# A two-layer decoder trunk on one core: other PSUM banks at a stage's end, one transposed piece and one small sum moved

## The chip, the cores and the metric

The kernel runs on one core of one Trainium2 chip. A core has TensorE (PE, with its weight loads shown as PEld), VectorE (DVE), ScalarE (ACT), GpSimd (POOL) and SyncE (SP), each with its own queue of instructions in a fixed order; they wait for each other by semaphores. Matmul results go to PSUM, which this kernel uses as eight banks of 128 x 512 float32. The metric is the time of one execution on the device, in microseconds (us).

## The reference

The input x has 256 tokens of 2048 channels, the memory 256 of the same width. All values are float32. Cut to what matters here:

```python
for i in range(2):
    if i == 1:                       # shared keys and values, from the stream after layer 0
        kv = rms_norm(x, kv_norm) @ w_kv
        k1, k2 = (partial_rope(rms_norm(k, k_norm)) for k in the first two column parts of kv)
        v = the rest of kv
    u = rms_norm(x, mix_norm[i]) @ w_in[i]
    if i == 0:  token_out = pooled means of u (windows 2, 4, 8, 16), one map for each group
    else:       token_out = differential attention of 12 heads with k1, k2, v
    q = rms_norm(the last 512 columns of u, by head)            # 4 memory heads of 128
    mem_out = softmax(q @ mem_k.T / sqrt(128)) @ mem_v           # for each head
    x = x + concat(token_out, mem_out) @ w_out[i]
    z = relu(rms_norm(x, ffn_norm[i]) @ w_ff1[i])                # 8192 wide
    x = x + (z * z) @ w_ff2[i]
```

## The kernel before

**Products.** Each float32 operand is split into a high part (rounded to fp32r) and a low part (the rest). A product is three matmuls: high by high, low by high, high by low. Weights come in rows of blocks in the order of use. `Feed` loads them (SP's queue), makes the high part with a cast on ScalarE (L199) and the low part with a subtraction on VectorE (L202), into a ring of slots, and does so up to three pieces of weights ahead of their use (`AHEAD`). A slot is free again when the matmuls that read it are done. The instructions of each engine are put in a fixed order before the run by a planner, which goes by the order of the program and by what it estimates to be ready.

**Small work between.** `at(d, fn)` puts a piece of work d steps ahead; `tick()` makes a step, after every four blocks of weights (a quad).

**Feed-forward stage** (`ffn`, once in each layer). 64 tiles of the first product (`up_tile`) go one after the other through the single bank of tag "st" (x_bank, copied out by L863). Between them stand jobs of the second product, computed with a scheme of seven products for two times two blocks; these hold the seven other banks: three of tag "mm", two of "s", one of "o", one of "t". When the left half of the output is done, it is turned back in four pieces (`turn_left`): four transposes into the "st" bank (L1020), a copy to SBUF (`evict`, L816), an add to the residual stream (L1028). `turns` holds the pieces; one is taken before each of the last up tiles, the fourth before tile 63. After tile 63, `last()` makes the last twelve jobs, eight, two and two of them ahead of output tiles 0, 1 and 2 (`down_tile`). After the last job, `finish_banks` combines the seven banks on VectorE (L1040 to L1048) and turns the right half back in four pieces (L1059, L1060). Output tiles 0 to 2 use the "st" bank, tiles 3 to 7 the three "mm" banks in turn; VectorE reads those from the bank (L891) and adds them (L892). As each chunk of the stream is finished, it is scaled and split into x_kv (L450 on ScalarE, L368 on VectorE).

**Keys and values.** Right behind, three tiles of keys and three of values are computed from x_kv, then two tiles for the memory. Each takes 16 steps, one for each chunk of x_kv; a step is `wide_step`, three products (L506, L507, L508) for each half of the tokens, and a bank for each half. `pair_of_banks(c, ...)` gives the two banks. The first key tile takes the chunks in the order `ready`, the others from 0 to 15.

**Queries of layer 1.** Three tiles of attention queries, and then four memory queries, one for each head. `mem_query` squares a head's query and, in `stats`, two steps later, sums the squares over the head's width by small matmuls into the "st" bank (L667); VectorE (L672) and ScalarE make the scale y of them. `mem_head` computes the scores four steps after the query, the exponentials with y (L699) and their scaling (L706), turns them four steps later (L712), and multiplies by the values after another four. The attention heads turn their outputs back through the "st" bank as well (`back`, L1545).

Of the kernel before, what the change touches and what calls it, by code (L numbers as in the profile page):

```python
# [10 lines left out]
F32 = mybir.dt.float32  # L11
# [6 lines left out]
P = 128  # L18
T = 256
NK = 16  # L20
# [310 lines left out]
def program(ctx, tc, plan, dry, xT, memT, par, lam, cst, wst, yT):  # L331
# [5 lines left out]
    pp = ctx.enter_context(tc.tile_pool(name="pp", bufs=1, space=PSUM))  # L337
# [10 lines left out]
    def at(d, fn, rank=1):  # L348
        pend.setdefault(now[0] + d, []).append((rank, fn))

    def tick():
        now[0] += 1
        for _, fn in sorted(pend.pop(now[0], []), key=lambda x: x[0]):
            fn()
# [6 lines left out]
    def vt(name):  # L361
        return tp.tile([P, T], F32, tag="v", bufs=6, name=name)

    def mmt(name):
        return pp.tile([P, 512], F32, tag="mm", bufs=3, name=name)

    def stt(out, a, s, b, op0, op1, **kw):
        return nc.vector.scalar_tensor_tensor(  # L368
            out=out, in0=a, scalar=s, in1=b, op0=op0, op1=op1, **kw
        )  # L370
# [44 lines left out]
    def gcol(c):  # L415
        return param[:, c : c + 1]
# [13 lines left out]
    def rsqrt_cols(out, v, parts=None):  # L430


        n = v.shape[-1]
        w = [tp.tile([P, 16], F32, tag="w8", bufs=8, name="rc")[:, :n] for _ in range(4)]
        if parts:
            for t in range(2):
                x, s, b = parts(t)
                nc.scalar.activation(w[0][:, t : t + 1], x, AF.Ln, scale=s, bias=b)
        else:
            nc.scalar.activation(w[0], v, AF.Ln)  # L440
        nc.scalar.activation(w[1], w[0], AF.Exp, bias=lnc, scale=-0.5)
        nc.vector.tensor_mul(w[2], w[1], w[1])
        nc.vector.tensor_mul(w[3], w[2], v)  # L443
        stt(out, w[3], 3.0 * CN * CN, w[1], ALU.subtract, ALU.mult, reverse0=True)

    def stat(name):
        return pp.tile([P, T], F32, tag="st", bufs=1, name=name)
# [64 lines left out]
    def b_tile(ps, w, l, c, xs):  # L512
        for k in range(NK):
            wide_step(ps, (w, l, k, c, 4), xs, k)

    def map_tile(ps, w, l, blocks, xs, ks=range(NK)):

        for k in ks:
            wide_step(ps, [(w, l, k, n, 1) for n in blocks], xs, k, ks)
# [132 lines left out]
    def mem_query(src, gq, cols):  # L652


        q = vt("mq")
        sq = vt("mq_sq")
        ql = tp.tile([P, T], F32R, tag="acc", bufs=1, name="mq_lo")
        q = q.bitcast(F32R)
        nc.scalar.activation(sq, src, AF.Square)
        nc.scalar.activation(q, src, AF.Copy, scale=gq)  # L660
        stt(ql, src, gq, q.bitcast(F32), ALU.mult, ALU.subtract)
        y = tp.tile([P, 2], F32, tag="m2", bufs=12, name="mq_y")

        def stats():
            st = stat("st_mq")
            for t in range(2):
                nc.tensor.matmul(  # L667
                    st[:, 2 * t : 2 * t + 2], sq[:, t * P : t * P + P], ones_h,
                    start=True, stop=True,
                )  # L670
            v2 = tp.tile([P, 2], F32, tag="m2", bufs=12, name="mq_v")
            nc.vector.tensor_mul(v2, st[:, 0:4].rearrange("p (a b) -> p a b", b=2)[:, :, 0], cols[1])  # L672
            nc.vector.tensor_scalar_add(v2, v2, EPS)
            rsqrt_cols(y, v2)
            nc.vector.tensor_mul(y, y, cols[0])

        at(2, stats)
        return (q, ql), y

    def mem_head(q, y, k, v, e, pT, out, lag, pv_lag=6, tag="s"):  # L680
# [88 lines left out]
    def ffn(l, xs, tags, done):  # L769
# [136 lines left out]
        def bank():  # L906
            return pp.tile([P, 512], F32, tag="st", bufs=1, name="x_bank")
# [13 lines left out]
        def slab_jobs(g, i, again, end):  # L921
            k = 2 * i
            first = 2 if g == 0 else 0
            n = feed.slab(
                [
                    [("w_ff2", l, k, c, 4), ("w_ff2", l, k + 1, c, 4)]
                    for c in (first, first + 1)
                ]
            )

            def side(b):
                assert i in done_pairs
                return [pair(i)[:, e, b * P : b * P + P] for e in range(2)]

            sides = (
                ((0, A11), (1, A12)),
                ((2, S1),),
                ((3, S2), (4, S4)),
                ((5, S3), (6, A22)),
            )  # L940

            def run(j):
                hi, lo = feed.job(n, j)
                for c, (p, a) in enumerate(sides[j]):
                    s = slice(512 * c, 512 * c + 512)
                    assert holds[p] == g
                    product(p, g, end, side(a), hi[:, s], lo[:, s])
                feed.job_used(n, j)
                if j == 3 and not again and i < 28:
                    pair_free[i % 5] = True  # L950

            return run
# [19 lines left out]
        def swap(j, g):  # L972
            for p in of_job[j]:
                x = keep.pop(0)
                nc.scalar.copy(x, banks[p])
                saved[1 - g, p] = x
                restore(p, g)

        left = {}
        turns = []  # L980
# [92 lines left out]
        jobs = [(s, j) for s in range(len(slabs)) for j in range(4)]  # L1073
        runs = {}

        def one_job():
            s, j = jobs.pop(0)
            g, i, again = slabs[s]
            end = s + 1 == len(slabs) or slabs[s + 1][0] != g
            if j == 0:  # L1080
                runs[s] = slab_jobs(g, i, again, end)
            runs[s](j)
            if end and s + 1 < len(slabs):
                if g == 1 and i == 27:
                    at(1, lambda: close_left(j))
                else:
                    at(3 if j == 3 else 2, lambda: swap(j, 1 - g))
# [7 lines left out]
        def due(tiles, least=0):  # L1095
            n = 0
            while len(jobs) > 12:
                s, j = jobs[0]
                if tiles_at(s) + j * (tiles_at(s + 1) - tiles_at(s)) / 4 > tiles and n >= least:
                    break  # L1100
                one_job()
                n += 1
# [5 lines left out]

        for i in range(4, 64):
            due(i, 2)  # L1110
            if turns:
                turn_left(turns.pop(0))
                due(i, 2)
            up_tile(i, bank(), lambda b, i=i: due(i + b / 16) if b > 0 and b % 4 == 0 else None)
        due(64)
        assert len(jobs) == 12 and not turns
        feed.loads_ahead = LOADS

        def last():
            for n in range(8):  # L1120
                for _ in range((8, 2, 2, 0, 0, 0, 0, 0)[n]):
                    one_job()
                    tick()
                if n == 2:
                    finish_banks()
                if n == 7:
                    feed.in_ffn, feed.more = False, None
                down_tile(n, bank() if n < 3 else mmt("ff2"))
# [80 lines left out]
    for i in range(2):  # L1209
        c = slice(2 * i, 2 * i + 2)  # L1210
# [21 lines left out]
    ps = [mmt("mq0"), pp.tile([P, 512], F32, tag="o", bufs=1, name="mq0")]  # L1232
# [12 lines left out]
    for i in range(2):  # L1245
        c = slice(2 * i, 2 * i + 2)
# [145 lines left out]
    nc.vector.tensor_scalar_mul(qcol, gcol(G_QN), 0.125)  # L1392

    def pair_of_banks(c, name):
        if c % 2:
            return [pp.tile([P, 512], F32, tag="s", bufs=2, name=name) for _ in range(2)]
        return [mmt(name) for _ in range(2)]

    c1 = []
    at(14, lambda: c1.extend(columns("x")))  # L1400
    for c in range(3):
        ps = pair_of_banks(c, "k1")
        ready = [0, 1, 2, 3, 4, 5, 8, 9, 10, 11, 6, 12, 13, 14, 15, 7] if c == 0 else range(NK)
        map_tile(ps, "w_kv", 0, (2 * c, 2 * c + 1, 6 + 2 * c, 7 + 2 * c), x_kv, ready)
        rows = key_rows(ps, c1, 64)
        rope(rows, ktab)
        for i in range(2):
            at(
                9,
                lambda i=i, c=c, rows=rows: turn_rows(  # L1410
                    rows, 2 * i, kT[:, 4 * c + 2 * i : 4 * c + 2 * i + 2, :], gcol(G_KN)
                ),
            )
    for c in range(3):
        ps = pair_of_banks(c + 1, "v1")
        b_tile(ps, "w_kv", 0, 3 + c, x_kv)
        for t in range(2):
            nc.scalar.activation(
                vv[c][:, t, :], ps[t], AF.Copy, scale=c1[0][:, t : t + 1]
            )  # L1420
# [3 lines left out]
    ps = pair_of_banks(0, "mk1")  # L1424
    b_tile(ps, "w_mem_kv", 1, 0, mems1)
    mrow1 = key_rows(ps, mem_c, P)
    ps = pair_of_banks(1, "mv1")
# [11 lines left out]
    for i in range(2):  # L1439
        c = slice(2 * i, 2 * i + 2)  # L1440
# [114 lines left out]
    for c in range(3):  # L1555
        ps = pair_of_banks(0, "q1")
# [4 lines left out]
        for i in range(2):  # L1561
            j = 2 * c + i
# [11 lines left out]
    for h in range(4):  # L1574
        ps = mmt("mq1")
# [106 lines left out]
```

## Time and profile before

| | |
|---|---|
| median of 3 runs | 2002.17 us (2001.77 to 2003.84) |
| profiled execution, its own time | 2003.26 us |
| its span, first to last instruction | 2001.5 us |
| mean granted TensorE clock | 0.999 |
| busy: PE, DVE, ACT, POOL | 1990.5, 1730.7, 1456.2, 157.7 us |
| read from HBM | 418.00 MB, 210 GB/s over the span |

Rows of the order of time give the start, the duration, the engine, the line, the operation, what it writes and reads with its shape, and how many instructions the row holds; in brackets stands how long the engine was idle just before, and which instruction ended that. A row of waits gives the engine and line that waited, the one waited for, and then the total in us, the number of times and the longest. Starts of neighbouring matmuls lie closer than their durations, since they overlap. A row by stretches ends with the granted clock, the share of DMA and GB/s.

### The profile page before, as it was taken

The numbers are of one execution on the slowest core, as the hardware profiler recorded it, in microseconds if no ns is written. First come the engines' busy times: TensorE is split into PE (matmuls) and PEld (weight loads), VectorE is DVE, ScalarE is ACT, GpSimd is POOL, SyncE is SP. The second block draws the span as 40 slices with busy tenths as digits, with TensorE's granted clock in tenths as the row PEclk, the third lists the DMA queues.
The fourth block names the chain that finished last, engine by engine and source line by source line (L and its number), as shares of the span: only waits on it lengthen the run. The fifth ranks groups of instructions, "written<-read, shape, count | busy, mean of one in ns | idle before, by whom it ended". The sixth has DMA issues, their size and how long they took to land.

```text
span 2001.5 us, 30206 instructions
## 1 busy us (share of the span) xinstructions
PE 1990.5 (99%) x10510; PEld 1699.4 (85%) x10510; DVE 1730.7 (86%) x2574; ACT 1456.2 (73%) x2316; POOL 157.7 (8%) x187
## 2 busy tenths in 40 slices
PE   9999999999999999999999999999999999999999
PEld 8888888888888888888888888888888888888888
DVE  8888778889989999999765698878889999899998
ACT  7765567687786878878665699557777777868875
POOL 0001210000000001000000000320000010000000
PEclk9999999999999999999999999999999999999999
DMA  9555587777778777755565533567777777787773
GB/s 320 172 187 192 185 237 214 229 221 236 220 231 241 220 225 231 226 177 168 180 236 194 179 127 123 200 211 226 224 216 235 231 233 227 226 240 220 232 232 110
DMA packets 145017, 422.08 MB, mean 211 GB/s; under 512 B 16352, under 2 KB 19040, under 8 KB 144864
## 3 DMA queue, kind: packets, MB, share of 16 engines
q1 hardware_dynamic: 127440, 388.69, 59.2%
q0 software_dynamic: 17280, 31.46, 9.2%
q8 instruction: 82, 1.34, 0.3%
q14 instruction: 71, 0.58, 0.1%
q10 hardware_dynamic: 144, 0.01, 0.0%
HBM read 418.00 MB, written 2.10 MB: 210 GB/s over the span
## 4 chain that ended last, share of the span: by engine, by line
PE 97%; DVE 1%; ACT 1%; issue 0%; DMA 0%; SPq 0%; DVEq 0%; ACTq 0%
PE x_bank L472 23%; PE x_bank L474 11%; PE p L919 9%; PE p L916 9%; PE p L918 9%; PE wo L472 6%; PE wo L474 3%; PE u L472 2%; PE ff L472 1%; PE u L474 1%; PE q L506 1%; PE k L506 1%; PE k L508 1%; PE q L508 1%; PE k L507 1%; PE v L508 1%
## 5 line engine op out<-in xcount | busy, mean ns | idle before, releaser
L199 ACT CAST hi_ring<-raw 128x512 fp32r<-128x512 f32 (+1 forms) x631 | 473.6, 756 | 232.8 <-DVE lo_ring L202 57.4
L202 DVE TENSOR_TENSOR lo_ring<-raw,hi_ring 128x512 fp32r<-128x512 f32 (+1 forms) x631 | 542.9, 868 | 113.4 <-ACT hi_ring L199 104.7
L472 PE MATMUL x_bank<-fx,hi_ring 128*128 128x512 f32 x1424 | 445.8, 394 | 1.4 <-ACT room L816 1.4
L202 DVE TENSOR_TENSOR lo_ring<-slab,hi_ring 128x1024 fp32r<-128x1024 f32 x222 | 270.3, 1221 | 64.4 <-ACT hi_ring L199 63.8
L199 ACT CAST hi_ring<-slab 128x1024 fp32r<-128x1024 f32 x222 | 232.6, 1052 | 125.7 <-PE x_bank L472 58.6
L474 PEld LDWEIGHTS x_bank<-fx,lo_ring 128*128 128x128 f32 x1424 | 267.0, 188 | 62.2 <-DVE lo_ring L202 1.9
L474 PE MATMUL x_bank<-fx,lo_ring 128*128 128x256 f32 x1424 | 280.9, 278 | 0.0
L472 PEld LDWEIGHTS x_bank<-fx,hi_ring 128*128 128x128 f32 x1424 | 233.4, 189 | 20.3 <-ACT room L816 1.8
L163 POOL DMA_DIRECT2D room<-in_w x120 | 103.8, 865 | 1138.3 <-DMA room<-in_w 1112.9
L916 PE MATMUL p<-hi_ring,z 128*128 128x512 f32 x444 | 173.8, 391 | 0.0
L918 PE MATMUL p<-hi_ring,z 128*128 128x512 f32 x444 | 173.5, 391 | 0.0
L919 PE MATMUL p<-lo_ring,z 128*128 128x512 f32 x444 | 172.0, 390 | 0.0
L472 PE MATMUL x_bank<-fx,zb 128*128 128x512 f32 x528 | 165.0, 394 | 0.0
L472 PE MATMUL wo<-cat,hi_ring 128*128 128x512 f32 x512 | 161.8, 397 | 0.3 <-DVE rc L443 0.3
L474 PEld LDWEIGHTS x_bank<-fx,zb 128*128 128x128 f32 x528 | 99.2, 188 | 22.4
L202 DVE TENSOR_TENSOR zb<-slab,zb 128x1024 fp32r<-128x1024 f32 x78 | 95.1, 1219 | 24.0 <-ACT zb L199 23.6
L474 PEld LDWEIGHTS wo<-cat,lo_ring 128*128 128x128 f32 x512 | 95.9, 188 | 22.0
L199 ACT CAST zb<-slab 128x1024 fp32r<-128x1024 f32 x78 | 82.2, 1053 | 41.2 <-PE x_bank L472 27.8
L474 PE MATMUL x_bank<-fx,zb 128*128 128x256 f32 x528 | 103.7, 278 | 0.0
L474 PE MATMUL wo<-cat,lo_ring 128*128 128x256 f32 x512 | 101.5, 279 | 0.0
L919 PEld LDWEIGHTS p<-lo_ring,z 128*128 128x128 f32 x444 | 83.3, 188 | 18.8 <-DVE lo_ring L202 0.8
L472 PEld LDWEIGHTS x_bank<-fx,zb 128*128 128x128 f32 x528 | 87.5, 189 | 7.5
(427 smaller groups left out, 4239.5 us busy)
## 6 DMA issues: line engine op xcount, KB each, us to landing
raw<-in_w SPq DMA_DIRECT2D x484, 512.0 KB, 4.2
slab<-in_w SPq DMA_DIRECT2D x120, 512.0 KB, 5.3
room<-in_w SPq DMA_DIRECT2D x180, 256.0 KB, 3.3
room<-in_w POOLq DMA_DIRECT2D x120, 256.0 KB, 6.2
slab<-in_w SPq DMA_DIRECT2D x60, 256.0 KB, 4.9
memraw<-in_mem SPq DMA_DIRECT2D x5, 512.0 KB, 4.5
resid<-in_x SPq DMA_DIRECT2D x8, 256.0 KB, 5.5
out_y<-resid SPq DMA_DIRECT2D x16, 128.0 KB, 1.9
```

The lines of the kernel that those rows point to most:

```text
L163: self.nc.gpsimd.dma_start(self.t1[i], right, accum_op=ALU.add)
L199: self.last_cast = self.nc.scalar.copy(hi, src)
L202: low = self.nc.vector.tensor_sub(lo, src, hi.bitcast(F32))
L472: nc.tensor.matmul(ps, hi, xs[:, k, :], start=first and c == 0, stop=False)
L474: nc.tensor.matmul(ps[:, T : 2 * T], lo, xs[:, k, 0:T], start=False, stop=last and c == len(ks) - 1,)
L506: nc.tensor.matmul(ps[t], x[t][1], hi, start=k == ks[0], stop=False)
L507: nc.tensor.matmul(ps[t], x[t][0], hi, start=False, stop=False)
L508: nc.tensor.matmul(ps[t], x[t][0], lo, start=False, stop=k == ks[-1])
L916: nc.tensor.matmul(ps, a[1], hi, start=new, stop=False, **again)
L918: nc.tensor.matmul(ps, a[0], hi, start=False, stop=False, **again)
L919: nc.tensor.matmul(ps, a[0], lo, start=False, stop=end, **again)
```

## The change

It does four things. `pair_of_banks` knows a third pair, the two single banks "o" and "t": the first and third key tiles take the "s" banks and the second the "mm" banks (before it was the other way round), the value tiles take "mm", "s" and the new pair (before "s", "mm", "s"). The first key tile takes chunk 5 after chunk 11 and chunk 6 ahead of chunk 7 at the end. The fourth piece of the left half is turned back not before up tile 63 but in `last()`, after the second of the eight jobs. And the sums of the memory queries come three steps after the query instead of two.

```diff
-        at(2, stats)
+        at(3, stats)
...
         for i in range(4, 64):
             due(i, 2)
-            if turns:
+            if turns and i < 63:
                 turn_left(turns.pop(0))
                 due(i, 2)
             up_tile(i, bank(), lambda b, i=i: due(i + b / 16) if b > 0 and b % 4 == 0 else None)
         due(64)
-        assert len(jobs) == 12 and not turns
+        assert len(jobs) == 12 and len(turns) < 2
         feed.loads_ahead = LOADS
 
         def last():
             for n in range(8):
-                for _ in range((8, 2, 2, 0, 0, 0, 0, 0)[n]):
+                for j in range((8, 2, 2, 0, 0, 0, 0, 0)[n]):
                     one_job()
+                    if turns and j == 1:
+                        turn_left(turns.pop(0))
                     tick()
...
     def pair_of_banks(c, name):
-        if c % 2:
+        if c == 2:
+            return [pp.tile([P, 512], F32, tag=tag, bufs=1, name=name) for tag in "ot"]
+        if c == 1:
             return [pp.tile([P, 512], F32, tag="s", bufs=2, name=name) for _ in range(2)]
         return [mmt(name) for _ in range(2)]
...
     for c in range(3):
-        ps = pair_of_banks(c, "k1")
-        ready = [0, 1, 2, 3, 4, 5, 8, 9, 10, 11, 6, 12, 13, 14, 15, 7] if c == 0 else range(NK)
+        ps = pair_of_banks(1 - c % 2, "k1")
+        ready = [0, 1, 2, 3, 4, 8, 9, 10, 11, 5, 12, 13, 14, 15, 6, 7] if c == 0 else range(NK)
...
     for c in range(3):
-        ps = pair_of_banks(c + 1, "v1")
+        ps = pair_of_banks(c, "v1")
```

## The prediction

> **What bounds the kernel now.** I read the page's busy shares and chain first, then who waited for whom on TensorE, then the order of time around each wait.
>
> ```profile
> PE 1990.5 (99%) x10510; PEld 1699.4 (85%) x10510; DVE 1730.7 (86%) x2574; ACT 1456.2 (73%) x2316; POOL 157.7 (8%) x187
> PE 97%; DVE 1%; ACT 1%; issue 0%; DMA 0%; SPq 0%; DVEq 0%; ACTq 0%
> PE k L506 <- DVE room L891: 2.9, 1, 2.9
> PE x_bank L472 <- ACT room L816: 1.4, 2, 0.7
> PE st_mq L667 <- DVE mq_y L368: 0.3, 1, 0.3
> ```
>
> TensorE is busy for 99% of the span and carries 97% of the chain; the change adds and removes no matmul. So it can only win TensorE's own stops, 11.0 us in all (2001.5 less 1990.5), and the slow clock behind them. Three of the stops are the ones it aims at: the first key tile (2.9), the fourth turned piece of either feed-forward stage (0.7 each), the memory query's sums (0.3). I take each by the order of time. I work against the profiled execution (2003.26, span 2001.5), 1.1 above the median of the runs, 2002.17; differences are carried over to the median. A measurement of this kernel can tell about 0.2%, 4 us, from no change.
>
> **The turned piece.** Feed-forward stage of layer 0, then of layer 1:
>
> ```profile
> 877.21 0.60 PE L1020 MATMUL x_bank<-const,room 128*128 128x128 f32 x4
> 877.84 0.59 ACT L816 COPY room<-x_bank 128x512 f32<-128x512 f32 x1 [0.79 <-PE x_bank L1020]
> 878.46 0.69 DVE L1028 TENSOR_TENSOR resid<-resid,room 128x512 f32<-128x512 f32 x1 [0.61 <-ACT room L816]
> 878.48 0.73 PE L472 MATMUL x_bank<-fx,hi_ring 128*128 128x512 f32 x2 [0.68 <-ACT room L816]
> 879.96 1.05 ACT L199 CAST hi_ring<-slab 128x1024 fp32r<-128x1024 f32 x1 [1.53 <-PE x_bank L472]
> 881.04 1.23 DVE L202 TENSOR_TENSOR lo_ring<-slab,hi_ring 128x1024 fp32r<-128x1024 f32 x1 [1.89 <-ACT hi_ring L199]
> 891.33 1.21 DVE L202 TENSOR_TENSOR zb<-slab,zb 128x1024 fp32r<-128x1024 f32 x1
> 892.60 0.73 PE L919 MATMUL p<-zb,z 128*128 128x512 f32 x2
> 1952.34 0.73 PE L472 MATMUL x_bank<-fx,hi_ring 128*128 128x512 f32 x2 [0.68 <-ACT room L816]
> ```
>
> The piece is four transposes, a copy out of the one "st" bank and an add; it issues no DMA, so SP's and POOL's queues are untouched. Tile 63 needs the same bank, so it starts 878.48 - 877.21 = 1.27 after the transposes did. Moved behind the second closing job, the transposes cost TensorE 0.60 there; the bank is free (tile 63's copy lies before) and is next wanted some microseconds later. The copy, 0.59, goes past ScalarE's casts into a stretch where it still has gaps (36.88 busy of 46.66 in the row below). TensorE alone: 0.60 - 1.27 = -0.67.
>
> But the add moves too, from a gap of VectorE (0.61 idle before it) into the stretch that follows:
>
> ```profile
> 881.04:927.70 46.66, 43.75 (x272) 38.59 (x270) 46.23 (x74) 36.88 (x60) 0.00 (x0) 1.00 0.34 108
> 1954.89:1992.57 37.68, 37.60 (x228) 33.20 (x227) 37.64 (x55) 25.68 (x34) 0.00 (x0) 1.00 0.27 87
> ```
>
> The columns are stretch, length, then busy time of TensorE, its weight loads, VectorE (46.23 of 46.66), ScalarE. From 881.04 VectorE has no free time. Its start hangs on TensorE (the cast at 879.96 waited for a slot that matmuls free, and VectorE for the cast), so it comes 1.27 earlier and grows by the add's 0.69: -0.58. TensorE already waits for VectorE inside it (zb at 891.33 lets the matmul at 892.60 go), so the smaller figure decides: **-0.6** in layer 0. Layer 1 has the same wait of 0.68 and the same full VectorE, and nothing behind but the output: **-0.6**. Ends: -0.67, and +0.69 if the stretch did not start earlier.
>
> **The key tile's banks and the order of chunks.** In order of time:
>
> ```profile
> 912.37 0.67 DVE L1046 TENSOR_TENSOR c_b<-c_b,p 128x512 f32<-128x512 f32 x1
> 923.19 0.68 DVE L202 TENSOR_TENSOR lo_ring<-raw,hi_ring 128x512 fp32r<-128x512 f32 x1
> 923.92 0.50 PE L508 MATMUL k<-lo_ring,x_kv 128*128 128x512 f32 x1
> 924.50 0.39 PE L507 MATMUL k<-hi_ring,x_kv 128*128 128x512 f32 x1
> 924.78 0.48 DVE L368 SCALAR_TENSOR_TENSOR x_kv<-resid,param,x_kv 128x256 fp32r<-128x256 f32 x1
> 925.78 1.66 DVE L368 SCALAR_TENSOR_TENSOR x_kv<-resid,param,x_kv 128x256 fp32r<-128x256 f32 x4
> 927.37 0.41 DVE L891 TENSOR_TENSOR room<-ff,r_x 128x256 f32<-128x256 f32 x1
> 927.70 0.68 DVE L202 TENSOR_TENSOR lo_ring<-raw,hi_ring 128x512 fp32r<-128x512 f32 x1
> 927.83 0.50 PE L506 MATMUL k<-hi_ring,x_kv 128*128 128x512 f32 x1 [2.95 <-DVE room L891]
> 928.17 0.39 PE L507 MATMUL k<-hi_ring,x_kv 128*128 128x512 f32 x1
> 928.40 0.63 PE L508 MATMUL k<-lo_ring,x_kv 128*128 128x512 f32 x2
> 929.12 0.63 PE L507 MATMUL k<-hi_ring,x_kv 128*128 128x512 f32 x1
> 930.45 1.29 DVE L202 TENSOR_TENSOR lo_ring<-raw,hi_ring 128x512 fp32r<-128x512 f32 x2
> 932.51 0.40 PE L506 MATMUL k<-hi_ring,x_kv 128*128 128x512 f32 x1
> 932.97 0.39 PE L508 MATMUL k<-lo_ring,x_kv 128*128 128x512 f32 x1
> 930.00:932.00 2.00, 2.00 (x6) 1.63 (x5) 2.00 (x5) 1.17 (x3) 0.00 (x0) 0.50 0.80 250
> ```
>
> The second half of k's first step waits for an "mm" bank that L891 of output tile 6 reads, 2.95. In the score banks that wait is gone: their last readers, the adds around 912.37, are done 11 us before. What is late next is the low part of the weights. The low part at 923.19 released the first step's L508 at 923.92; the next, for the second step, is the one at 927.70, ready at 927.70 + 0.68 = 928.38. VectorE comes to it so late because chunk 5, chunks 12 to 15 and L891 stand ahead of it in program order, and neither the banks nor the order in which TensorE takes the chunks changes that order. So TensorE issues the rest of step one and the first products of step two (both halves' high products at best), and then stops at step two's L508 until 928.38, or 927.8 with the 0.6 from above. Before, five products were left at 928.40: L508 of either half-step, then L506, L507, L508. Afterwards four are left, or two if the high products went ahead: 1 to 3 products of 0.23 (928.17 to 928.40), 0.23 to 0.69. I take the middle: **-0.45**.
>
> The gap stays about as long (three to five more products after 924.50 end at 925.4 to 925.9, and 928.4 ends it), and with it what came after: between 929.12 and 932.51 eight products took 3.39 at a granted clock of 0.50, against 8 x 0.23 = 1.84, so 1.55 lost. I leave it lost. At full clock the bound is the low parts at 930.45, the first of which ends at 931.13 and feeds step four: TensorE used it at 932.97, so 1.8 is the most that can be won with VectorE's order as it is. Without any wait it would be 2.95 + 1.55 = 4.5. Ends: 0 and -4.5; the row nearest to it is the low part at 927.70.
>
> The Trainium skill, "TensorE: Matmul & The Clock Gate", section "Why this matters for your kernels", asks only for no idle gaps over about 3 us, beyond which the clock halves. This trace does not agree: a gap of 2.95 was enough. By that rule the new gap, if shorter, would leave the clock up; that is the second rival.
>
> The new order of chunks costs nothing: chunk 5 is written at 924.78, long before either place. Of the later tiles none waits for a bank in the list of TensorE's waits, and each bank has a whole tile between its uses, the two single banks too. Zero; they are covered by a tile of matmuls each.
>
> **The memory query's sums one quad later.** They share the one "st" bank with the heads' turn-backs.
>
> ```profile
> 1200.69 0.61 PE L667 MATMUL st_mq<-ones_h,mq_sq 128*128 128x2 f32 x4
> 1220.24 0.58 PE L667 MATMUL st_mq<-ones_h,mq_sq 128*128 128x2 f32 x4 [0.35 <-DVE mq_y L368]
> 1230.22 0.50 PE L667 MATMUL st_mq<-ones_h,mq_sq 128*128 128x2 f32 x4
> 1207.57 0.14 DVE L672 TENSOR_TENSOR mq_v<-st_mq,d_x 128x2 f32<-128x2 f32 x1
> 1213.36 0.92 ACT L706 ACTIVATE att<-att,mm_rec 128x256 f32<-128x256 f32 x2
> 1214.68 0.60 PE L712 MATMUL mt<-const,att 128*128 128x128 f32 x4
> 1223.53 0.91 ACT L706 ACTIVATE att<-att,mm_rec 128x256 f32<-128x256 f32 x2
> 1225.34 0.60 PE L712 MATMUL mt<-const,att 128*128 128x128 f32 x4
> ```
>
> The third wait, 0.35, goes: what it waits for has a quad more time. Behind the sums hang L672, two small ScalarE steps, y, the exponentials and the transposes L712, with 0.40 to spare in the first head (1213.36 + 0.92 to 1214.68) and 0.90 in the second. A quad is (1230.22 - 1200.69) / 12 = 2.46, so a chain that slipped by all of it would stop TensorE. Also, in the third and fourth head the sums now fall into the quad of a turn-back and queue behind it on the bank. Ends: -0.35, and +2.06 and +1.56 in the first two heads. I take **0**: the wait won is given back; it is nearest to the row of 0.35.
>
> **Sum.** -0.6 - 0.45 - 0.6 + 0 = -1.65: 2001.6 against the profiled 2003.26, 2000.5 on the median.
>
> **The rivals.**
> - *The clock stays up.* The gap in the key tile falls so that the clock does not halve. Against it: the trace's own 2.95. For it: the gap may be shorter. Then 1.8 instead of 0.45: -3.0, 1999.2.
> - *VectorE's order changes.* The order is planned anew for the changed program; if the low part of 927.70 moves ahead of the four x_kv writes at 925.78, the stop shrinks to under 1 us and the clock stays: -0.6 - 4.5 - 0.6 - 0.35 = -6.05, 1996.1. For it: nothing in these rows holds the low part back but its place in the line. Against: before, VectorE kept to program order here.
> - *The moved add takes back the turned piece.* If VectorE's stretch is not started by TensorE, it only grows: +0.69 in layer 0 and about 0 in layer 1, less 0.45: 2002.4. Against it: the 1.53 that names TensorE.
> - *The sums come too late.* They slip by a whole quad behind the turn-backs, and L712 stops TensorE by 2.06 + 1.56, and in the third head by about their mean, 1.8: +5.4 on the sum, 2005.9. It decides once the chains slip by more than 0.6 (mean slack) + 1.65/3, about 1.2 each. For it: 0.40 of slack. Against: L672 came 6.9 after its sums (1200.69 to 1207.57), almost three quads, so the sums did not hold the chain.
>
> **Numbers.** Forecast 0.50, clock 0.14, VectorE's order 0.18, the add 0.08, the sums 0.10. Range 1996.0 to 2003.2: it leaves out the last case and the edges of the others. Faster by over 0.2% (below 1998.2): the third case and a little of the second, 0.20. Slower by over 0.2% (above 2006.2): half of the last, 0.05. Within: 0.75.
>
> **What would show it.** No wait of k on L891; instead a wait of k's second step on a low part, 2.5 to 3 us, with a granted clock near 0.5 behind it. No wait of tile 63 on L816, and L1028 inside VectorE's full stretch. No wait at the third sums. Wrong if the low part of step two stands ahead of the x_kv writes, if the clock stays at 1.0 after the gap, or if L712 waits.

## The result, and the profile after

The kernel after takes 2000.18 us (median of 22 runs, 1999.32 to 2001.80), the kernel before in the same series 2003.74 (22 runs): ratio 0.9984, 95% interval 0.9978 to 0.9991. That is faster, but by less than the 0.2% named in the prediction. The two profiled executions differ by 3.02 (2003.26 and 2000.24; spans 2001.5 and 1998.5). The forecast was -1.65, so the gain is about twice the forecast. That 2000.5 nevertheless stands beside 2000.18 is partly chance: it was counted from the median of the 3 runs shown, 2002.17, which lies 1.6 below that of the 22.

The page of the kernel after: busy times, then the chain by engine. TensorE's busy time has not changed by a tenth; all that went is standing time, 11.0 before and 8.0 now.

```profile
PE 1990.5 (100%) x10510; PEld 1700.2 (85%) x10510; DVE 1729.9 (87%) x2574; ACT 1455.0 (73%) x2316; POOL 157.3 (8%) x187
PE 98%; ACT 1%; DVE 0%; issue 0%; DMA 0%; SPq 0%; ACTq 0%; DVEq 0%
```

TensorE's waits, first those of before that the prediction did not show, then the whole list of after:

```profile
PE warm L413 <- PEq L1655: 0.8, 1, 0.8
PE mk L499 <- DVE mems L1173: 0.7, 1, 0.7
PE wo L472 <- DVE rc L443: 0.3, 1, 0.3
```

```profile
PE k L508 <- DVE lo_ring L202: 2.7, 1, 2.7
PE warm L413 <- PEq L1659: 0.8, 1, 0.8
```

The waits on the copy L816 (1.4), on the memory query (0.3) and on rc (0.3) are gone; so is that of mk at the start, which the change does not touch and which came back at 0.2 to 0.8 in other executions. The key tile still waits, 2.7 against 2.9 before, but for the low part of the weights and no longer for the bank.

The kernel after in order of time: the turned piece of layer 0, then the key tile.

```profile
879.87 1.22 DVE L202 TENSOR_TENSOR lo_ring<-slab,hi_ring 128x1024 fp32r<-128x1024 f32 x1 [1.80 <-ACT hi_ring L199]
885.06 0.60 PE L1020 MATMUL x_bank<-const,room 128*128 128x128 f32 x4
885.41 0.47 PE L916 MATMUL p<-zb 128*128 128x512 f32 x1
887.48 0.69 DVE L1028 TENSOR_TENSOR resid<-resid,room 128x512 f32<-128x512 f32 x1
...
924.68 0.39 PE L507 MATMUL k<-hi_ring,x_kv 128*128 128x512 f32 x1
925.09 1.68 DVE L368 SCALAR_TENSOR_TENSOR x_kv<-resid,param,x_kv 128x256 fp32r<-128x256 f32 x4
926.69 0.42 DVE L891 TENSOR_TENSOR room<-ff,r_x 128x256 f32<-128x256 f32 x1
927.02 0.68 DVE L202 TENSOR_TENSOR lo_ring<-raw,hi_ring 128x512 fp32r<-128x512 f32 x1
927.76 1.22 PE L508 MATMUL k<-lo_ring,x_kv 128*128 128x512 f32 x2 [2.69 <-DVE lo_ring L202]
```

All four transposes stand between closing jobs and take 0.35 from their start to that of the next product (885.06 to 885.41), although their row says 0.60. The add stands in VectorE's stretch. In the key tile the four high products of step two go ahead and the last is at 924.68; then TensorE waits 2.69, behind x_kv and L891 in VectorE's line.

**Where the time went.** The rest is read by stages, each from the start of one product to the start of another, so that the start of the program (the first product p lies between 274.0 and 274.9) falls out. The marks are the first p of layer 0 (L916), the last k (L508), the last ff of layer 1's first up tiles (L474) and the last ff of the span (L488); in the kernel before and in the kernel after:

```profile
274.13 0.40 PE L916 MATMUL p<-hi_ring,z 128*128 128x512 f32 x1
...
995.80 0.39 PE L508 MATMUL k<-lo_ring,x_kv 128*128 128x512 f32 x1
...
1342.16 0.40 PE L474 MATMUL ff<-fx,lo_ring 128*128 128x256 f32 x2
...
1997.13 0.28 PE L488 MATMUL ff<-z,lo_ring 128*128 128x256 f32 x1
```

```profile
274.32 0.40 PE L916 MATMUL p<-hi_ring,z 128*128 128x512 f32 x1
...
994.48 0.39 PE L508 MATMUL k<-lo_ring,x_kv 128*128 128x512 f32 x1
...
1340.08 0.40 PE L474 MATMUL ff<-fx,lo_ring 128*128 128x256 f32 x2
...
1994.12 0.28 PE L488 MATMUL ff<-z,lo_ring 128*128 128x256 f32 x1
```

Their differences, in us, one profiled execution for each kernel:

| kernel | p to last k | k to ff | ff to the end | clock halved behind k's stop |
|---|---|---|---|---|
| before | 721.67 | 346.36 | 654.97 | yes |
| after | 720.16 | 345.60 | 654.04 | yes |
| turned piece alone | 720.43 | 346.32 | 654.07 | yes |
| banks and order alone | 721.50 | 346.31 | 654.94 | yes |
| sums alone | 720.49 | 345.49 | 654.84 | no |
| after, old order | 720.44 | 345.54 | 653.97 | yes |
| after, five quads ahead | 717.94 | 345.50 | 654.02 | no |
| after, four quads ahead | 719.09 | 345.54 | 653.99 | no |
| after, stop filled | 719.24 | 345.55 | 654.03 | no |
| after, second add | 720.54 | 345.53 | 654.00 | no |
| after again, 1st, 2nd, 3rd | 720.24, 720.18, 719.74 | 345.55, 345.57, 345.56 | 653.94, 653.94, 653.97 | yes, yes, no |
| before, five quads ahead | 721.51 | 346.32 | 654.89 | yes |

After less before: -1.51, -0.76 and -0.93, and +0.19 from a later start: -3.0. In the last two columns, kernels whose code is the same in a stage agree within 0.13. The first column holds the slow clock too, and two kernels can be compared there only where it fell alike.

### The profile page after: what moved, and what is told of

The parts are those of the page before. It is cut to its first block, busy times and chain, and to the rows that moved or that the text cites. A ratio compares the mean times of both kernels' runs of the same rounds, so it can differ in the third digit from the quotient of the medians.

```text
span 1998.5 us, 30202 instructions
## 1 busy us (share of the span) xinstructions
PE 1990.5 (100%) x10510; PEld 1700.2 (85%) x10510; DVE 1729.9 (87%) x2574; ACT 1455.0 (73%) x2316; POOL 157.3 (8%) x187
## 4 chain that ended last, share of the span: by engine, by line
PE 98%; ACT 1%; DVE 0%; issue 0%; DMA 0%; SPq 0%; ACTq 0%; DVEq 0%
PE x_bank L472 23%; PE x_bank L474 11%; PE p L916 9%; PE p L918 9%; PE p L919 9%; PE wo L472 6%; PE wo L474 3%; PE u L472 2%; PE ff L472 1%; PE u L474 1%; PE q L506 1%; PE k L508 1%; PE q L508 1%; PE q L507 1%; PE v L506 1%; PE v L507 1%
## 5 line engine op out<-in xcount | busy, mean ns | idle before, releaser
L474 PEld LDWEIGHTS x_bank<-fx,lo_ring 128*128 128x128 f32 x1424 | 267.0, 188 | 62.2 <-DVE lo_ring L202 1.9
L474 PE MATMUL x_bank<-fx,lo_ring 128*128 128x256 f32 x1424 | 280.8, 278 | 0.0
L916 PE MATMUL p<-hi_ring,z 128*128 128x512 f32 x444 | 173.8, 391 | 0.0
L474 PEld LDWEIGHTS x_bank<-fx,zb 128*128 128x128 f32 x528 | 99.1, 188 | 22.5
L474 PEld LDWEIGHTS wo<-cat,lo_ring 128*128 128x128 f32 x512 | 95.9, 188 | 22.3
L474 PE MATMUL x_bank<-fx,zb 128*128 128x256 f32 x528 | 103.7, 278 | 0.0
L474 PE MATMUL wo<-cat,lo_ring 128*128 128x256 f32 x512 | 101.0, 278 | 0.0
```

Of the source, the lines that this page charges most:

```text
L474: nc.tensor.matmul(ps[:, T : 2 * T], lo, xs[:, k, 0:T], start=False, stop=last and c == len(ks) - 1,)
L916: nc.tensor.matmul(ps, a[1], hi, start=new, stop=False, **again)
```

## Experiments

Theory: the three parts act alone and add up, and VectorE's line holds k's second step. Rivals: the bank held it; the moved add takes its gain back; the sums come too late; the clock, not the stop, is the price in the key tile.

**1. The turned piece alone.**

```diff
-            if turns:
+            if turns and i < 63:
                 turn_left(turns.pop(0))
...
+                    if turns and j == 1:
+                        turn_left(turns.pop(0))
```

> The kernel before with the moved turned piece alone. Prediction on record: -0.6 in either layer, -1.2 on the span (2000.3 against 2001.5). Reading of the trace after: VectorE's stretch in layer 0 starts 1.37 earlier (1.17 and the 0.2 by which that run started late) and its add takes 0.60 from start to start, so k resumes 0.77 earlier; in layer 1 TensorE wins some 1.0 and nothing behind it gives it back: -1.8 together. In layer 0 TensorE should be about 1.0 ahead at the last product of the down-projection before k, and k's wait for L891 should grow by the difference (2.95 to about 3.2). Rival: the add in VectorE's full stretch takes the gain back in both layers: 0 or a little slower.

Measured: 2002.35 against 2003.39, ratio 0.9995 (0.9986 to 1.0003), which alone could not be told from no change; the stages can: -1.24 to the last k and -0.90 in layer 1. VectorE in this kernel, and in the kernel before the one row that is missing here:

```profile
879.65 1.23 DVE L202 TENSOR_TENSOR lo_ring<-slab,hi_ring 128x1024 fp32r<-128x1024 f32 x1 [1.80 <-ACT hi_ring L199]
916.09 0.48 DVE L368 SCALAR_TENSOR_TENSOR x_kv<-resid,param,x_kv 128x256 fp32r<-128x256 f32 x1
926.67 0.68 DVE L202 TENSOR_TENSOR lo_ring<-raw,hi_ring 128x512 fp32r<-128x512 f32 x1
```

```profile
917.11 0.48 DVE L368 SCALAR_TENSOR_TENSOR x_kv<-resid,param,x_kv 128x256 fp32r<-128x256 f32 x1 [0.33 <-ACT x_kv L450]
```

The stretch starts 1.39 earlier (881.04 before), the add in it costs about 0.60 from start to start, and a wait of 0.33 of VectorE for ScalarE at 917.11 is no longer there: 1.39 - 0.60 + 0.33 = 1.12, and the low part at 927.70 came 1.03 earlier. The other 0.2 of the 1.24 is the clock. It was halved here from about 926.34 (means of 0.67, 0.50, 0.50 and 0.63 in the four stretches of 1 us from 926), 0.47 before k went on at 926.81; in the kernel before it was halved from about 929.06, after k had gone on. The 0.47 that fell into the stop cost nothing, and half of it, 0.24, is won. So the moved piece itself is worth about 1.0 in layer 0. The wait on L891 was 2.96 against 2.95, not 0.25 longer: the bank comes earlier by as much as TensorE does. The rival falls in both layers.

**2. Banks and order of chunks alone.**

```diff
-        ps = pair_of_banks(c, "k1")
+        ps = pair_of_banks(1 - c % 2, "k1")
```

and with it the new `pair_of_banks`, `ready` and the value tiles' pairs.

> The kernel before with the new banks for k and v and the new order of chunks alone. Prediction on record: -0.45; the wait on L891 turns into a wait of 2.5 to 3 us on the low part of step two, and the clock stays near 0.5 for 3.4 us behind it. Reading of the trace after: three products of 0.23 ahead, -0.7. Rival (the bank was what held k): 2.95 of stop and 1.55 of slow clock go, -4.5.

Measured: 2003.05 against 2003.39, ratio 0.9999 (0.9991 to 1.0008); -0.17 to the last k. VectorE in this kernel, and then TensorE's wait:

```profile
926.47 0.42 DVE L891 TENSOR_TENSOR room<-ff,r_x 128x256 f32<-128x256 f32 x1
926.81 0.87 DVE L368 SCALAR_TENSOR_TENSOR x_kv<-resid,param,x_kv 128x256 fp32r<-128x256 f32 x2
927.60 0.42 DVE L892 TENSOR_TENSOR resid<-resid,room 128x256 f32<-128x256 f32 x1
927.93 1.29 DVE L202 TENSOR_TENSOR lo_ring<-raw,hi_ring 128x512 fp32r<-128x512 f32 x2
```

```profile
PE k L508 <- DVE lo_ring L202: 2.9, 1, 2.9
```

The rival falls: without the bank's wait there is one of the same length on the low part. Less came out than either reading said, because the planner put L892 ahead of the low part: 927.93 instead of 927.70, and 0.36 later counted from the first p. That takes back half of the three products (0.69) that go ahead; of the 0.33 left, 0.16 did not show, and these rows do not say why.

**3. The sums alone.**

```diff
-        at(2, stats)
+        at(3, stats)
```

> The kernel before with the memory query's sums one quad later alone. Prediction on record: 0, the wait of 0.35 is given back elsewhere. Reading of the trace after: the stage between the last mq product of x_mx and the last wo product is 0.75 shorter, no wait of st_mq on mq_y and none of wo on the rc of L443, so -0.75. Rival: the sums come too late and L712 waits, up to +5.4.

Measured: 2002.67 against 2003.39, ratio 0.9997 (0.9988 to 1.0006); the stage from k to ff is 0.87 shorter, and two stops of the kernel before are gone:

```profile
1220.24 0.58 PE L667 MATMUL st_mq<-ones_h,mq_sq 128*128 128x2 f32 x4 [0.35 <-DVE mq_y L368]
1229.67 0.47 PE L472 MATMUL wo<-cat,hi_ring 128*128 128x512 f32 x1 [0.34 <-DVE rc L443]
```

Here the third and fourth sums lie at 1222.75 and 1232.79, neither waits, and L712 does not either. So what was won was kept, and there was a second stop to win, at 1229.67. The rest of the 0.87, about 0.2, is not accounted for by waits. The difference of 1.18 before the last k is no effect of the sums, which come later: the clock stayed up in this execution (see 8).

**4. The old order of chunks in the kernel after.**

```diff
-        ready = [0, 1, 2, 3, 4, 8, 9, 10, 11, 5, 12, 13, 14, 15, 6, 7] if c == 0 else range(NK)
+        ready = [0, 1, 2, 3, 4, 5, 8, 9, 10, 11, 6, 12, 13, 14, 15, 7] if c == 0 else range(NK)
```

> The kernel after, but k's first tile takes the chunks of x_kv in the old order (5 after 4, 6 before 12). Prediction on record: the order of the chunks is worth 0, since chunk 5 is written before either place. So the wait of 2.7 on the low part of step two and all later times stay within 0.2 of those of the kernel after. Rival: chunk 5 in the sixth place, or 6 in the eleventh, comes too late and TensorE waits for x_kv there; then it loses what the kernel after won, 0.5 to 1.

Measured: 2000.30, the wait 2.7 as with the new order, the other stages within 0.07. To the last k it took 0.28 more, a little above the 0.2 named. About 0.1 of this is the clock: in the kernel after it was halved from about 927.56, 0.2 before k went on, here from about 928.9, after k had gone on. Against the first repetition of the kernel after (720.24, see 8), where it was also halved only behind the stop, 0.2 stays. VectorE came to the low part of step two 0.14 later than in the kernel after, counted from the first p, which is most of it. So in these single executions the new order is worth about 0.2; the medians do not tell it apart. No wait for x_kv, so the rival falls.

**5 and 6. Weights split further ahead around the key tile.** The limit of pieces split ahead of their use is raised from output tile 6 until the first key tile has been issued (the last line stands behind its `map_tile`), to five or to four:

```diff
-        while self.pp < min(i + 1 + AHEAD, len(self.plan.prep)):
+        while self.pp < min(i + 1 + self.ahead, len(self.plan.prep)):
...
+                if n == 6:
+                    feed.ahead = 5
...
+        feed.ahead = AHEAD
```

> The kernel after, with weights for k split up to five quads ahead instead of three until k's first tile has been issued, so that in VectorE's line the low parts of steps two and three stand ahead of chunks 5 and 12 to 15. Theory (VectorE's place in line holds k): the wait of 2.7 on the low part of step two goes; the low parts of steps two and three are there at about 924.5, TensorE does those steps and stops first at the low part of step four, at about 928.8, for about 1.1 us: twelve products of 0.23 ahead less 1.0 of later start, -1.7, and -1.5 more where the clock does not halve behind so short a gap: -1.7 to -3.3 against the kernel after. Rival: VectorE is full, so what is moved up only moves the stop: a stop of 2.5 or more elsewhere, 0 within 0.3.

> The same with four quads ahead: the low part of step two alone stands ahead of the chunks. Theory: the stop is at the low part of step three, at about 928.0, for about 1.75 us; six products of 0.23 ahead less 0.28: -1.1, and -1.5 more where the clock does not halve. Rival as for five quads: 0 within 0.3.

Measured: 1997.99 with five (8 runs; ratio to before 0.9973, 0.9962 to 0.9983), 1998.79 with four (0.9976, 0.9968 to 0.9985); against the 2000.18 of the kernel after -2.2 and -1.4. The clock stayed up in both. Against an execution of the kernel after in which it also stayed up (719.74 to the last k, see 8), five win 1.80 and four 0.65, and this is what the place in line is worth by itself. With five, in order of time, in the numbering of that kernel (L203 makes the low part, L369 x_kv, L509 the product with it), then the wait:

```profile
923.57 1.29 DVE L203 TENSOR_TENSOR lo_ring<-raw,hi_ring 128x512 fp32r<-128x512 f32 x2
924.77 0.48 DVE L369 SCALAR_TENSOR_TENSOR x_kv<-resid,param,x_kv 128x256 fp32r<-128x256 f32 x1
925.17 1.28 DVE L1061 TENSOR_TENSOR resid<-resid,ct 128x512 f32<-128x512 f32 x2
926.43 1.69 DVE L369 SCALAR_TENSOR_TENSOR x_kv<-resid,param,x_kv 128x256 fp32r<-128x256 f32 x4
927.73 0.39 PE L508 MATMUL k<-hi_ring,x_kv 128*128 128x512 f32 x1
928.37 0.68 DVE L203 TENSOR_TENSOR lo_ring<-raw,hi_ring 128x512 fp32r<-128x512 f32 x1
929.11 0.72 PE L509 MATMUL k<-lo_ring,x_kv 128*128 128x512 f32 x2 [0.98 <-DVE lo_ring L203]
```

```profile
PE k L509 <- DVE lo_ring L203: 1.0, 1, 1.0
PE tc_x L541 <- DVE acc L757: 0.3, 1, 0.3
```

Both low parts stand ahead of chunk 5 and of the four writes, and TensorE comes to a stop only at step four, for 0.98. With four the stop is 1.7, at step three. Theory shown: it was VectorE's place in line. The 1.5 more that was expected where the clock stays up came only in part (see 8). The rival (the same stop elsewhere) falls.

**7. A second add behind the moved one.**

```diff
                 nc.vector.tensor_add(resid[:, c : c + 2, :], resid[:, c : c + 2, :], two)
+                if late:
+                    nc.vector.tensor_add(x, x, x)
```

`late` is true for the moved piece only.

> The kernel after with one more add of 128x512 on VectorE behind the moved piece's own, in either layer; it changes nothing in the result. Theory (in layer 0 VectorE's line sets when k goes on, in layer 1 TensorE alone sets the end): the low part of step two and k's second step come 0.60 later in layer 0, 0.3 if the wait of VectorE for ScalarE at about 917 gives way; in layer 1 the last product of the span stays where it is against the end of layer 0's k tile. Rival: VectorE binds in both layers (0.6 later in either), or in neither (0).

Measured in one profiled execution: the low part of step two at 927.64, which is 0.81 later counted from the first p, and the stage from ff to the end 654.00 against 654.04. The clock stayed up behind the stop of 2.9 (the third number from the end):

```profile
930.00:932.00 2.00, 2.00 (x11) 1.63 (x10) 2.00 (x6) 1.66 (x4) 0.00 (x0) 1.00 0.72 260
```

To the last k it took 0.80 more than the execution of the kernel after in which the clock also stayed up (720.54 against 719.74, see 8). So VectorE's line counts in layer 0 and costs nothing in layer 1. The 0.81 is more than the 0.60 of the add: VectorE also waited 0.42 for ScalarE before an x_kv write, where the kernel after did not.

**8. Is it the stop that halves the clock?** First the stop filled with ten products nobody reads, behind k's first step:

```diff
+            if w == "w_kv" and blocks[0] == 0 and k == ks[0]:
+                idle = pp.tile([P, 512], F32, tag="st", bufs=1, name="idle")
+                for _ in range(10):
+                    nc.tensor.matmul(idle, xs[:, 0, 0:P], xs[:, 0, :], start=True, stop=True)
```

> The kernel after with ten products of 128x512 whose result nobody reads, put into k's stop behind its first step; TensorE is then idle for under 1 us there. Theory (the gap halves the clock): the granted clock stays at 1.0 behind it, k's second step goes on at the same time, and the 1.0 to 1.5 us that the slow clock cost is won: -1.0 to -1.5 against those runs of the kernel after that had the slow clock, somewhat less in the median, because the kernel with the sums alone had a gap of 3.0 with the clock at 1.0 behind it. Rival: the slow clock does not depend on the gap, or the low parts behind it bind: 0, or up to +0.5 because the ten products end too late.

Measured: 1999.24 (ratio to before 0.9980, 0.9971 to 0.9989), 0.9 under the kernel after; its remaining stop is 0.4. Then the kernel after itself, three times more:

> The kernel after itself, one more profiled execution (the first of three). Question: does the slow clock belong to the gap of 2.7 before k's second step, or does it come and go? If the gap decides (a threshold between 1.75 and 2.7), every execution shows the clock at 0.5 for about 3.4 us behind it and k's last product 720.2 after the first product p. If it comes and goes with the same gap, some executions show 1.0 throughout, and in them k's last product comes 0.6 to 1.3 earlier, less a wait of 0.3 to 0.8 on VectorE that the kernels with the clock up showed behind it.

> The kernel after itself, the second of three, with the same expectations as the first.

> The kernel after itself, the third of three, with the same expectations as the first.

All three show the wait of 2.69. Rows by stretches, the granted clock third from the end: the first, then the third, then the one with the filled stop.

```profile
928.00:930.00 2.00, 1.71 (x7) 1.41 (x8) 2.00 (x6) 1.34 (x3) 0.00 (x0) 0.94 0.00 0
930.00:932.00 2.00, 2.00 (x7) 1.52 (x6) 1.91 (x5) 1.47 (x4) 0.00 (x0) 0.50 0.74 262
932.00:934.00 2.00, 2.00 (x8) 1.62 (x7) 2.00 (x6) 2.00 (x6) 0.00 (x0) 0.71 0.71 264
```

```profile
928.00:930.00 2.00, 2.00 (x10) 1.61 (x9) 2.00 (x6) 1.49 (x5) 0.00 (x0) 1.00 0.30 106
930.00:932.00 2.00, 2.00 (x11) 1.62 (x10) 2.00 (x6) 2.00 (x7) 0.00 (x0) 1.00 0.64 213
```

```profile
928.00:930.00 2.00, 2.00 (x10) 1.59 (x10) 2.00 (x6) 1.47 (x4) 0.00 (x0) 1.00 0.20 27
```

With the very same stop the clock halved twice and stayed up once. And staying up is worth little: 719.74 against 720.18 and 720.24 to the last k, 0.45 to 0.5, because of what is late next. The third execution's TensorE:

```profile
945.34 0.61 PE L540 MATMUL tc_x<-ones_d,acc 128*128 128x2 f32 x4 [0.76 <-DVE acc L756]
```

The sums of tc_x (the sums of squares for the scale of the keys) wait for VectorE's adds L756 as soon as the key tile no longer comes late; with the clock halved they do not. So the 1.0 to 1.5 expected of the filled stop came to 0.9, and the clock is only half of that: the filled stop is 0.50 ahead of this third execution too, because tc_x waits 0.27 there and not 0.76. VectorE was held up less by casts of ScalarE ahead of it; why, no run here shows.

**9. Splitting further ahead without the new banks.** The edit of 5 on the kernel before.

> The kernel before with weights split five quads ahead, as in the faster version, but with the old banks, the old turned piece and the old sums. Theory (the banks are what lets TensorE use low parts that are there earlier): k's second half still waits for L891 of output tile 6, which now stands behind two more low parts on VectorE and comes about 1.2 later; TensorE has six more products of the first half to do before it stops, 1.4; so -0.2, and the stop on L891 stays about 3 us. Rival (the low parts alone held k, the bank does not matter): the stop shrinks to 1 and the kernel wins about 2 as the version with the new banks did.

Measured: 2002.87 against 2003.57, ratio 0.9994 (0.9985 to 1.0003); to the last k 721.51 against 721.67, -0.16.

```profile
PE k L507 <- DVE room L892: 2.5, 1, 2.5
```

As the theory said, the bank still stops k, now at 2.5 instead of 2.9. So either block alone hides the other: the banks alone brought 0.17, the low parts alone 0.16, and both (with the turned piece) 3.73 to the last k, of which the turned piece alone brings 1.24. In the 2.5 that are left the clock has a share, since it stayed up only in the execution with both.

## Why the prediction was right, and where its terms were off

*Turned piece: mechanism right, size wrong.* Forecast -0.6 and -0.6, measured -1.24 and -0.90; 0.24 of the first is luck with the clock. Two sizes failed, and in layer 1 also the step "the smaller figure decides". TensorE's own term was 0.60 - 1.27; the transposes cost 0.35 from start to start, so 0.35 - 1.27 = -0.92, and that is layer 1 to 0.02. VectorE's term was -1.27 + 0.69; the add costs 0.60, and the sentence "From 881.04 VectorE has no free time" was wrong by the row quoted with it: 46.23 of 46.66 leaves 0.43, of which the wait at 917.11 took 0.33, and the add went there in part. VectorE does decide in layer 0: the second add put k off by 0.8. In layer 1 VectorE does not decide at all: the second add moved nothing there.

*Key tile: right in kind.* The wait moved from L891 to the low part, 2.7 long, three products ahead, and the clock was halved in the profiled execution. In one of four executions of this kernel it stayed up behind the same stop, which the prediction had named as a sign of being wrong. Forecast -0.45; alone -0.17, and on top of the turned piece -0.27 (1.51 - 1.24). Alone, VectorE's order was planned anew and put one more add (L892) ahead of the low part, which took back 0.36. In the kernel after that add stands behind the low part, and there the clock hides part of the gain: without what fell into the stops (0.24 and 0.10) the turned piece alone wins 1.00 and the whole change 1.41 to the last k, which leaves about 0.4 for the banks and the order. The order of chunks, forecast at zero, has about 0.2 of this.

*Memory query's sums: wrong.* Forecast 0, measured -0.76 in the kernel after and -0.87 alone. The step that failed is "the wait won is given back". The prediction itself had the row that spoke against it (L672 comes 6.9 after its sums, so the sums hold nothing up), and the wait of wo on rc, 0.34, stood one line below those it quoted in the list of TensorE's waits and was not asked about.

*The sum.* The turned piece gave 0.94 more than forecast (0.24 of it by the clock), the sums 0.76 more, the key tile 0.18 less: 1.52 on top of the 1.65, so 3.17, and with a start 0.19 later than before that is the 3.0 of the two spans. The 3.56 of the medians is 0.5 more; the profiled execution of before lies 0.5 under its median, the one of after 0.06 above.

*The rivals.* The clock that stays up was priced at 1.35 (1.8 instead of 0.45); it stays up in some executions and is worth 0.45 to 0.5 in the profiled ones, since tc_x waits next. VectorE's new order did come about, in other places than the low part; where it was made to (5), the key tile won 2.2 more, not the 4.05 (4.5 less 0.45) that this rival gave it, with a stop of 0.98 at step four and one of 0.35 before tc_x left. The add that takes the gain back and the sums that come too late did not occur.

## What to carry to other kernels

Price a moved instruction by the distance from its start to that of the next one in a full stretch, not by its row's duration, and read the free time of a "full" engine to the last tenth: both errors here had the same sign. When two things hold one instruction (a bank and a low part), taking away either brings next to nothing (0.17 and 0.16 here) and says nothing against it; look at what stands ahead in the other engine's line, and move that as well. Before the difference of two single executions is put down to a change, look where the slow clock lay in either. And ask of every line in the list of waits whether the change reaches it, the small ones too.

## What the runs showed of the hardware

A stop of TensorE does not halve the clock by its length alone. Behind stops of 2.5 to 3.0 the granted clock fell to 0.5 in 8 of 11 profiled executions and stayed at 1.0 in 3 (the sums alone, the second add, the third repetition); the shortest stop behind which it fell was 2.53 (experiment 9). With stops of 0.4, 1.0 and 1.7 (one execution each) it stayed up. Where it fell, it did so for 3.4 us in each of the eight, as worked out from the means in stretches of 2 us (0.94, 0.50 and 0.71 in the first repetition give 929.8 to 933.2), beginning between 0.5 before the end of the stop and 1.5 after it.

The Trainium skill, "TensorE: Matmul & The Clock Gate", section "What's actually happening", describes a free-running window of about 3.4 us and a clock that falls after at least one idle window. The length agrees with the 3.4 seen here, and a window with a phase of its own would explain why the same stop of 2.69 does and does not halve the clock; that no full idle window is needed is shown by the eight stops, all shorter than 3.4. Where the limit lies, and that it is the phase, no run here shows.

The mean granted clock over a whole run points the same way. It is 1.000 in all 19 runs with four or five quads ahead; in the 22 of the kernel after it is 1.000 in 8, 0.999 in 13 and 0.998 in 1. A clock halved for 3.4 us takes 0.0009 off that mean. The 8 runs take 1999.7 on average and the 13 take 2000.6, so a clock that stays up may be worth more than the 0.45 to 0.5 of the profiled executions; where it was low in the runs without a profile is not recorded, and the mean is coarse (the profiled execution with the filled stop has 0.999, although the clock stayed up behind its stop).
